# A row-wise NaN maximum: the second tile's load in four strided DMAs, one of them ahead of the first tile's

## Chip, cores and metric

The kernel runs on one core of a Trainium2 chip. The metric is the device time of one execution in microseconds; the runs give the median of several.

## What is computed

The input is 32 x 2048 x 2048 float32 numbers (512 MiB), of which about a tenth are NaN. The output is the maximum of each row of 2048 numbers with NaNs left out, 65536 numbers in all.

```python
batch, seq, dim = 32, 2048, 2048
x = np.random.randn(batch, seq, dim).astype(np.float32)
mask = np.random.rand(batch, seq, dim) < 0.1
x[mask] = np.nan

def reference(x, axis):          # axis = -1
    return np.nanmax(x, axis=axis).astype(np.float32)
```

## The kernel before

The 65536 rows are cut into six groups of tiles (`GROUPS`, from the list `TILES`). In a group each of the 128 partitions holds consecutive rows of the input. A tile is given in quarters of a row (`Q` = 512 numbers, 2 KB): the first tile of the kernel has 4 quarters in each partition (one row, 8 KB, 1 MB in all), the second and nearly all others have 28 (seven rows, 56 KB in each partition, 7 MB in all); the last tiles are cut finer. Three buffers `xt0` to `xt2` take turns.

Each tile goes through four steps. SyncE loads it by one or more DMAs (`load`, line 246). ScalarE reads the upper halfwords of the numbers and writes 16-bit keys to a buffer `kt` (line 270). GpSimd, or now and then ScalarE, turns the keys back into halfwords in which a NaN has become a very low number, and writes them over the old ones in `xt` (lines 280 and 270). VectorE takes the maximum of each row (`tensor_reduce`, line 287). A tile is cut into two or three pieces for this, so that the steps of one tile overlap.

The order on each engine is written out by the program, and the class `Order` places the semaphores: `add` gives an instruction the waits that it needs and an event (a semaphore's name and its count) that others can wait for. A DMA adds 16 to its semaphore. `load` takes one of 14 semaphores (`LANES`) in turn, and a load into a buffer waits until VectorE has read the tile that was in it.

The first three loads, one for each buffer, wait for nothing. They are issued in a block of their own (lines 255 to 264) ahead of the main part, one DMA over all 128 partitions each, and their events stand in the list `ahead`. The main loop takes an event out of `ahead` for each of the first three tiles and issues loads of its own from the fourth on. ScalarE's first piece of a tile waits for the event of its load.

At the end the maxima are stored by six DMAs (line 503).

Of the kernel before, what the change touches and what calls it, by code (L numbers as in the profile page):

```python
# [184 lines left out]
def kernel(  # L185
# [15 lines left out]
    nc = tc.nc  # L201
# [28 lines left out]
    def maxima(lo, hi):  # L230

        if hi <= early:
            return acc0[:, lo:hi]
        assert lo >= early
        return acc1[:, lo - early : hi - early]

    order = Order(nc)
    lanes = [[] for _ in range(LANES)]
    turn = 0

    def load(out, source, deps):
        nonlocal turn
        e = order.add(
            "sp",
            nc.sync,
            lambda: nc.sync.dma_start(out=out, in_=source),  # L246
            deps + lanes[turn],
            lane=f"load{turn}",
            step=16,
        )  # L250
        lanes[turn] = [e]
        turn = (turn + 1) % LANES
        return e

    with tc.tile_critical():  # L255
        xg = xr[P * rows[-1] : P * (rows[-1] + rows[0])].rearrange("(p s) d -> p (s d)", p=P)
        ahead = []
        base = 0
        for xt, ((c,), _, _) in zip(xts, GROUPS[0]):
            c *= Q  # L260
            ahead.append(load(xt[:, :c], xg[:, base : base + c], []))
            base += c
    tc.close()
    tc.compile()  # L264

# [10 lines left out]
    def pool(deps, pair=None, **kw):  # L276
        return order.add(
            "pool",
            nc.gpsimd,
            lambda: nc.gpsimd.tensor_scalar(**kw),  # L280
            deps,
            lane=pair,
            joint=pair is not None,
        )

    def dve(deps, do, **kw):
        return order.add("dve", nc.vector, lambda: do(**kw), deps)  # L287

    def find(deps, acc):
        return dve(  # L290
            deps,
            nc.vector.scalar_tensor_tensor,
            out=acc,
            in0=acc,
            scalar=LEAST,
            in1=acc,
            op0=ALU.is_ge,
            op1=ALU.mult,
        )

    def find_late(deps, acc, none):
        e = pool(
            deps,
            out=none,
            in0=acc,
            scalar1=LEAST,
            scalar2=float(0x00400000),
            op0=ALU.is_lt,
            op1=ALU.mult,
        )  # L310
        bits = acc.bitcast(i32)
        return order.add(
            "pool",
            nc.gpsimd,
            lambda: nc.gpsimd.tensor_tensor(out=bits, in0=bits, in1=none, op=ALU.add),  # L315
            [e],
        )
# [19 lines left out]
    for gi, (s, g) in enumerate(zip(rows, GROUPS)):  # L337
        if gi == len(GROUPS) - 1:
            r0 = 0
        xg = xr[r0 : r0 + P * s].rearrange("(p s) d -> p (s d)", p=P)  # L340
        og = of[r0 : r0 + P * s].rearrange("(p s) -> p s", p=P)
        r0 += P * s
        first = sum(rows[:gi])
        acc = maxima(first, first + s)
        base = 0
        for loads, pieces, reds in g:
            assert sum(loads) == total(pieces) == sum(reds)
            xt, before = xts[number % BUFS], free[number % BUFS]
            number += 1
            landed = []  # L350
            at = 0
            for c in loads:
                c *= Q
                if ahead:
                    e = ahead.pop(0)
                else:
                    e = load(xt[:, at : at + c], xg[:, base + at : base + at + c], before)
                landed.append((at, at + c, e))
                at += c
            clean = []  # L360
            after = []
            at = done = 0
# [27 lines left out]
            def name(i):  # L390
                return f"pair{number}_{pairs[i][0]}" if i in pairs else None
# [15 lines left out]
            for parts in pieces:  # L407
                parts = parts if isinstance(parts, tuple) else (parts,)
                c = int(sum(map(abs, parts))) * Q
                here = [l for a, b, l in landed if a < at + c and b > at]  # L410
                kold = []
                if used + c > KEYS:
# [9 lines left out]
                    out=kts[key][:, used : used + c],  # L422
                    in_=xt[:, at : at + c].bitcast(i16)[:, 1::2],
# [6 lines left out]
                for c in parts:  # L430
                    on = more.pop(0)
                    back, wait, c = c < 0, isinstance(c, float), int(abs(c)) * Q
# [7 lines left out]
                    else:  # L440
                        group.append((at - c, used - c, key))
                        if not on:
                            assert all(k == key for _, _, k in group)
                            lo, klo, _ = group[0]
                            e = pool(
                                [e_key],
                                name(piece),
                                out=xt[:, lo:at].bitcast(i16)[:, 1::2],
                                in0=kts[key][:, klo:used],
                                scalar1=-1.0,  # L450
                                scalar2=float(TOP),
                                op0=ALU.mult,
                                op1=ALU.add,
# [5 lines left out]
                    while reds and done + reds[0] <= min([at] + open_):  # L459
# [8 lines left out]
                        else:  # L468
                            m = max(n // D, 1)
                            to = acc[:, row : row + m]  # L470
                        e = dve(
                            [e for a, b, e in clean if b > lo and a < done] + part,
                            nc.vector.tensor_reduce,
                            out=to,
                            in_=xt[:, lo:done]
                            .bitcast(f32)
                            .rearrange("p (c d) -> p c d", c=m),
                            axis=mybir.AxisListType.X,
                            op=ALU.max,
# [13 lines left out]
        else:  # L493
            e = find(after, maxima(lo, flagged))
            ready += [e] * (gi + 1 - len(ready))
        if gi == len(GROUPS) - 1:
            e = find_late(late_after, late_acc, late)
            ready[LATE] = e
    for (og, bits), e in zip(stores, ready):
# [5 lines left out]
            lane="store",  # L505
            step=16,
# [38 lines left out]
```

## Time and profile before

| what | value |
|---|---|
| time, median of 3 runs | 1250.57 us (1250.36 to 1250.6) |
| span of the profiled execution, first to last instruction | 1248.8 us |
| time of that execution beyond its span | not given by the profile; the median is 1.77 us above the span |
| VectorE (DVE) busy | 1110.5 us, 89% |
| ScalarE (ACT) busy | 968.8 us, 78% |
| GpSimd (POOL) busy | 1164.9 us, 93% |
| DMA queue of the loads, share of 16 engines | 537.14 MB, 99.6% |

The profile is one execution. A row of a timeline has the start, the time taken, the engine, the line, the operation, its output and input, and in brackets the idle time of the engine before it with what ended it. The chain is the work that ended last, followed back from the end; a row of it has the start, the length and what it was. A row of the waits says who waited for whom: total time, number, longest. A row of the windows has the stretch, its length, the busy time of VectorE, ScalarE and GpSimd with instruction counts, the granted clock, the share of time in which the 16 DMA engines were busy, and GB/s. A packet's bytes are counted in the window in which it starts, so very short windows jump. A row of the DMA issues has the count, the KB of one and the time from issue to landing.

### The profile page before, as it was taken

To read this page: it belongs to the slowest core of one execution; us is meant where nothing else is said; L and a number is where in the kernel's file an instruction comes from. 1 tells how busy PE (TensorE), PEld (TensorE's weight loads), DVE (VectorE), ACT (ScalarE), POOL (GpSimd) and SP (SyncE) were. 2 spreads that over 40 slices of the span, in tenths; PEclk is the share of its full clock that TensorE was granted. 3 is DMA by queue.
4 is the path that set the end of the run, shared out by engine and by line. 5 is a ranking of instruction groups with operands and counts; after the bars stand their busy time and mean duration, and the time that the engine had idled before them with its cause. 6 is when DMAs were issued, how large, how long until landed. Compare 5 with 4: busy or idle time off the path is not lost.

```text
span 1248.8 us, 884 instructions
## 1 busy us (share of the span) xinstructions
DVE 1110.5 (89%) x181; ACT 968.8 (78%) x280; POOL 1164.9 (93%) x238
## 2 busy tenths in 40 slices
DVE  0888989888889888898988888988888989999999
ACT  3777887778777877788777877777777779989998
POOL 2999989998999899998999899999999999999998
DMA  9999999999999999999999999999999999999998
GB/s 416 441 413 439 441 441 425 428 441 441 428 425 441 441 435 417 441 441 439 426 428 441 439 432 422 441 441 435 419 439 441 435 430 432 429 432 427 431 428 326
DMA packets 16855, 537.20 MB, mean 430 GB/s; under 512 B 2640, under 2 KB 2640, under 8 KB 4944
## 3 DMA queue, kind: packets, MB, share of 16 engines
q1 hardware_dynamic: 16848, 537.14, 99.6%
q14 instruction: 7, 0.06, 0.0%
HBM read 536.87 MB, written 0.26 MB: 430 GB/s over the span
## 4 chain that ended last, share of the span: by engine, by line
DVE 38%; DMA 36%; POOL 17%; ACT 9%; issue 1%; SPq 0%
DMA xt<-in_x_dram 36%; DVE acc L287 22%; POOL xt L280 17%; DVE lead L287 16%; ACT kt L270 8%; ACT xt L270 1%; SPq L246 0%; SPq L264 0%; SPq L255 0%
## 5 line engine op out<-in xcount | busy, mean ns | idle before, releaser
L280 POOL TENSOR_SCALAR xt<-kt 128x6144 int16<-128x6144 uint16 (+9 forms) x232 | 1163.8, 5016 | 80.5 <-ACT kt L270 67.1
L270 ACT ACTIVATE kt<-xt 128x3584 uint16<-128x3584 int16 (+10 forms) x248 | 913.0, 3720 | 271.8 <-DMA xt<-in_x_dram 250.3
L287 DVE TENSOR_REDUCE acc<-xt 128x3 f32<-128x6144 f32 (+3 forms) x119 | 896.2, 7571 | 132.9 <-POOL xt L280 125.6
L287 DVE TENSOR_REDUCE lead<-xt 128x1 f32<-128x2048 f32 (+3 forms) x59 | 212.9, 3690 | 0.5 <-POOL xt L280 0.5
L270 ACT ACTIVATE xt<-kt 128x512 int16<-128x512 uint16 (+4 forms) x30 | 57.1, 1913 | 0.6
L270 ACT ACT_TABLE_LOAD x1 | 1.3, 1283 | 3.3 <-PEq L264 3.3
L319 DVE MEMSET lead<- 128x1 f32 x1 | 0.1, 59 | 3.4 <-PEq L264 3.4
L287 DVE SCALAR_TENSOR_TENSOR acc<-acc 128x414 f32<-128x414 f32 x1 | 1.2, 1178 | 0.0
L280 POOL TENSOR_SCALAR lead<-lead 128x91 int32<-128x91 f32 x1 | 0.6, 551 | 0.1
L315 POOL TENSOR_TENSOR lead<-lead 128x91 int32<-128x91 int32 x1 | 0.4, 376 | 0.1
L526 POOL MEMSET const-float32-0.0<- 128x1 f32 x1 | 0.1, 99 | 0.2 <-issue 0.2
L270 ACT ACTIVATE lead<-lead 128x1 f32<-128x1 f32 x1 | 0.2, 203 | 0.0
L287 DVE SCALAR_TENSOR_TENSOR lead<-lead 128x7 f32<-128x7 f32 x1 | 0.2, 168 | 0.0
L526 POOL MEMSET const-bfloat16-1.0<- 128x1 bf16 x1 | 0.1, 102 | 0.0
L526 POOL MEMSET const-uint8-127<- 128x1 uint8 x1 | 0.1, 102 | 0.0
L526 POOL MEMSET const-float32-1.0<- 128x1 f32 x1 | 0.1, 99 | 0.0
## 6 DMA issues: line engine op xcount, KB each, us to landing
xt<-in_x_dram SPq DMA_DIRECT2D x61, 7168.0 KB, 22.6
xt<-in_x_dram SPq DMA_DIRECT2D x3, 4096.0 KB, 18.6
xt<-in_x_dram SPq DMA_DIRECT2D x5, 2048.0 KB, 27.5
xt<-in_x_dram SPq DMA_DIRECT2D x3, 3072.0 KB, 25.5
xt<-in_x_dram SPq DMA_DIRECT2D x2, 4352.0 KB, 16.5
xt<-in_x_dram SPq DMA_DIRECT2D x3, 2816.0 KB, 23.3
xt<-in_x_dram SPq DMA_DIRECT2D x2, 3584.0 KB, 25.2
xt<-in_x_dram SPq DMA_DIRECT2D x5, 1024.0 KB, 27.6
```

The source lines that it names most:

```text
L270: lambda: nc.scalar.activation(**kw),
L280: lambda: nc.gpsimd.tensor_scalar(**kw),
L287: return order.add("dve", nc.vector, lambda: do(**kw), deps)
L315: lambda: nc.gpsimd.tensor_tensor(out=bits, in0=bits, in1=none, op=ALU.add),
L319: e_warm = order.add("dve", nc.vector, lambda: nc.vector.memset(warm, 1.0), [])
L526: nc = _bacc.Bacc("TRN2", target_bir_lowering=False, num_devices=1)
```

## The change

The second tile's load becomes four DMAs over strided partitions: partitions 0, 8, 16, ... (16 rows of 56 KB), 4, 12, 20, ... (16 rows), 2, 6, 10, ... (32 rows) and 1, 3, 5, ... (64 rows). The first of them is issued in front of the first tile's load, the other three behind it, and then the third tile's load as before. A helper `first` issues the four; they share one semaphore, and the event that stands in `ahead` for the second tile is the last one's (count 64), so that whoever waits for it waits for all four. Bytes, buffers and everything after these loads stay as they were.

```diff
+    def first(out, source):
+        return order.add(
+            "sp",
+            nc.sync,
+            lambda: nc.sync.dma_start(out=out, in_=source),
+            [],
+            lane="first",
+            step=16,
+        )
...
         ahead = []
         base = 0
+        heads = []
         for xt, ((c,), _, _) in zip(xts, GROUPS[0]):
             c *= Q
-            ahead.append(load(xt[:, :c], xg[:, base : base + c], []))
+            heads.append((xt[:, :c], xg[:, base : base + c]))
             base += c
+        first(*[a[0::8] for a in heads[1]])
+        ahead.append(load(*heads[0], []))
+        for at, step in ((4, 8), (2, 4), (1, 2)):
+            e = first(*[a[at::step] for a in heads[1]])
+        ahead.append(e)
+        ahead.append(load(*heads[2], []))
```

## The prediction

> **What bounds the kernel now.** I read the page from the top: span, engines, the slices, the DMA queues.
>
> ```profile
> span 1248.8 us, 884 instructions
> DVE 1110.5 (89%) x181; ACT 968.8 (78%) x280; POOL 1164.9 (93%) x238
> DMA  9999999999999999999999999999999999999998
> q1 hardware_dynamic: 16848, 537.14, 99.6%
> ```
>
> The 16 DMA engines are busy for 99.6% of the span. No compute engine is, though POOL's 93% is near. Busy shares are averages, so the stretches come next, with the DMA share and GB/s last in each row.
>
> ```profile
> 100.00:400.00 300.00, 267.63 (x37) 227.69 (x56) 284.97 (x52) 1.00 1.00 434
> 400.00:800.00 400.00, 357.79 (x48) 306.51 (x74) 379.68 (x69) 1.00 1.00 435
> 1100.00:1200.00 100.00, 100.00 (x26) 91.78 (x37) 89.97 (x25) 1.00 1.00 430
> 1200.00:1240.00 40.00, 40.00 (x19) 39.63 (x35) 38.31 (x20) 1.00 1.01 422
> ```
>
> The stream runs at 434 GB/s from end to end: its rate is the kernel's rate. VectorE is full as well from 1100 us. What started that run is in the chain of waits that ended last; behind it stands the row of the waits that says how tiles begin.
>
> ```profile
> 999.14 21.81 DMA xt<-in_x_dram
> 1020.95 0.02 issue
> 1020.97 5.33 ACT kt L270
> ...
> 1040.75 33.88 DVE lead L287 x8
> ...
> 1079.63 163.72 DVE lead L287 x49
> ```
> ```profile
> ACT kt L270 <- DMA xt<-in_x_dram: 250.3, 62, 15.0
> ```
>
> VectorE's closing run hangs on a landing at 1020.95 us, and ScalarE waited 62 times for a landing, so tiles start when their data come. Every landing from the second tile on stands behind the second tile's bytes in one full stream. If those bytes take X longer, all later landings, and the end, move by X. The same holds for a gain. The question is what the altered front of the stream costs or saves.
>
> **The front as it is.** The chain in the first 60 us gives SyncE's three issues; the DMA issues of the first 50 us give time to landing; ScalarE's timeline gives its first pieces.
>
> ```profile
> 0.95 0.37 SPq L246
> ...
> 1.38 0.42 SPq L246
> ...
> 1.85 37.53 DMA xt<-in_x_dram
> 39.39 0.02 issue
> 39.41 3.20 ACT kt L270
> ```
> ```profile
> xt<-in_x_dram SPq DMA_DIRECT2D x1, 1024.0 KB, 4.6
> ```
> ```profile
> 5.55 1.91 ACT L270 ACTIVATE kt<-xt 128x2048 uint16<-128x2048 int16 x1 [0.76 <-DMA xt<-in_x_dram]
> 22.47 3.19 ACT L270 ACTIVATE kt<-xt 128x3584 uint16<-128x3584 int16 x1 [15.01 <-DMA xt<-in_x_dram]
> ```
>
> Issues go out at 0.95, 1.38 and 1.85 us. The first tile lands at 0.95 + 4.6 = 5.55, the second at about 22.45, the third at 39.39 us. The last two are 7168 KB apart: 39.39 - 22.45 = 16.94 us, or 433 GB/s. Shared by 16 engines, each moves its 8 of the 128 partition rows (56 KB each) in 16.94 us, **2.12 us a row**. The first tile's 1024 KB would take 2.42 us at that rate.
>
> Short windows show the slow start.
>
> ```profile
> 0.00:1.90 1.90, 0.00 (x0) 0.00 (x0) 0.20 (x4) 1.00 0.00 0
> 1.90:2.50 0.60, 0.00 (x0) 0.00 (x0) 0.00 (x0) 1.00 1.19 232
> 2.50:3.00 0.50, 0.00 (x0) 0.00 (x0) 0.00 (x0) 1.00 0.80 295
> 5.00:22.00 17.00, 2.29 (x1) 1.91 (x1) 2.46 (x1) 1.00 1.00 435
> ```
>
> No byte moves before 1.90 us. Then 0.60 us at 232 instead of 435 GB/s loses 0.60 x (1 - 232/435) = 0.28 us, and 0.50 us at 295 loses 0.16 us: **0.44 us** in all.
>
> **The change part by part.**
>
> *The first issue.* It still goes out at about 0.95 us, but asks for 16 rows of 56 KB in place of 128 rows of 8 KB: one long row for each engine, if all 16 take part. Long rows may cover the slow first reads; at best all 0.44 us come back, at worst none, and the stagger could grow by as much. I take a gain of 0.2 us, half of what is lost. The issue itself took 1.0 us to first byte (0.95 to about 1.95) for 128 rows; nothing in the trace shows that fewer rows shorten this, and more than the 1.0 us cannot be saved.
>
> *Three more issues.* By the two rows above one takes 0.37 to 0.42 us plus some 0.05 us between them. Six instead of three end at about 0.95 + 6 x 0.47 = 3.8 us. The queue then holds at least 0.9 MB of the first strided DMA and 1 MB of the first tile, over 4 us of work from 1.95 us, so the DMA engines don't run dry. If the cover were gone, the price would be three issues, 1.4 us. Completion counts of three more DMAs are a few tiny writes; I cost them at nothing.
>
> *The first tile moves back* by 0.43 us of issue, and its bytes stand behind 16 rows: its landing goes from 5.55 to some 7.5 to 10 us. Behind it are ScalarE's first piece (idle 15.01 us after it), POOL's and VectorE's, and SyncE's next issue, the fourth tile's, which waits for VectorE to release the buffer:
>
> ```profile
> 10.04 2.29 DVE L287 TENSOR_REDUCE acc<-xt 128x1 f32<-128x2048 f32 x1 [6.62 <-POOL xt L280]
> 12.36 0.33 SPq L246 DMA_DIRECT2D xt<-in_x_dram  x1
> ```
>
> Issued at 12.36 us, it isn't served before the third tile is in, at 39.39 us. Moved to some 17 us it keeps over 20 us of cover; nothing is lost. The second tile's pieces now wait for all four DMAs; before, they waited for all of one. No other queue is passed: POOL and ScalarE issue no DMA.
>
> *The same 7168 KB in 16, 16, 32 and 64 rows.* This is the disputed term. Every load in the trace goes over 128 partitions. That each of 16 engines runs 27 GB/s beside the 15 others may be the engine's limit or that of the place in the on-chip memory that it writes to; with 128 rows the two can't be told apart, as each engine may have a place to itself. With every 8th partition, 16 engines write 16 rows in an order that no row of the trace covers. Lower bound: the limit is the engine's, 2.12 us a row, cost 0. Upper bound: throughout the 128 rows two engines share the room of one, 4.24 us a row; each engine has 1 + 1 + 2 + 4 = 8 rows, cost 8 x 2.12 = 16.94 us. I take sharing for the two 16-row DMAs and none for the other two: one row per engine, 8 partitions apart, is furthest from the 128-row loads, while 32 and 64 rows still step finely over the whole width and are nearest to them. Cost: 2 x 2.12 = **4.2 us**.
>
> [...]
>
> Sum: -0.2 + 4.2 = +4.0 us. The profiled span of 1248.8 us becomes 1252.8. The median of the runs, 1250.57, lies 1.77 us above that span; the page has no other time for that execution, and I keep these 1.77 us. **Forecast: 1254.6 us.**
>
> **The rivals.** 0.2% is 2.5 us, about what a measurement of this kernel can tell from no change; slower then means above 1253.1, faster below 1248.1 us.
>
> *A, nothing is shared.* The limit is the engine's and 16 engines take part in each DMA. Only the start changes: -0.2 us, 1250.4 us (1250.1 to 1251.0). For it: the steady 434 GB/s over every stretch, which looks like a fixed engine rate. Against it: each of those rows has the same 128-partition shape. It decides from the point where two 16-row DMAs together cost under 2.7 us instead of 4.2 us: then the kernel is not slower by my bound.
>
> *B, all four are shared.* If the rows of the 32- and 64-row DMAs are dealt out in consecutive runs, two per engine and four per engine, then neighbouring engines start 8 partitions apart there too, as in the 16-row DMAs, and walk in step. Cost 16.94 - 0.2: 1267.3 us. If only the 32-row DMA joins, it is two more rows, 4.2 us: 1258.8; if only the 64-row one joins, 8.5 us: 1263.1. For it: the engines start their rows together, and two that share are slowed alike and stay in step. Against it: nothing shows how rows are dealt out, and the 64-row DMA steps only two partitions.
>
> *C, fewer engines.* The DMAs over 16 rows don't use all engines. If eight carry two rows each in both, they fall 2 x 2.12 = 4.2 us behind the others, and a load counts as landed only with its last row. That is the forecast's time by another way. If the first DMA loads one half and the third issue the other, all engines stay level: that is A. [...]
>
> *D, faster.* This needs 2.5 us, but the start has 0.44 us lost rate and 1.0 us of issue latency, and the stream is otherwise full. Only a rate above 434 GB/s for strided rows would do it, and nothing in the trace goes there.
>
> **How the numbers follow.** Forecast, C included: 0.38, its own range 1253.5 to 1256.0 (no startup gain and a stagger as large on top, or a part of the second shared DMA overlapped by rows of its neighbours). A: 0.21. B: 0.38, about two thirds of it with all four shared. D: 0.03. No case but D may be left out if 8 in 10 are to be held, so the range runs from A's lower end to B's upper end: 1250.0 to 1267.6 us. Slower by over 0.2%: forecast and B, 0.76. Within: A, 0.21. Faster: D, 0.03.
>
> **What would show it.** In the timeline after, ScalarE's piece on the second tile should start at about 26.5 us instead of 22.47, and the third tile's about 16.94 us behind it, at 43.4. The first tile's piece should start near 9.8 us; at 7.5 us it says that 16 rows took the plain 2.12 us, which is A. Short windows of the DMA should show about half of 435 GB/s where the 16-row DMAs run and 435 elsewhere; half of it for over 30 us is B. SyncE's six issues should end before 4 us, with no gap in the stream. From 100 us on, all rows should be as before, moved by the same amount. A second tile that lands late without the end moving by as much would break the step that carries the delay 1:1; a changed rate in the middle of the kernel would break the whole account.

## The result and the profile after

The changed kernel takes **1255.45 us** (median, 1255.42 to 1255.71); the kernel before, run beside it, takes 1250.43 us. The ratio is 1.0041, 95% interval [1.003, 1.0052]: slower by 5.0 us, where 4.0 us was forecast (1254.6 us).

The page of the changed kernel:

```profile
span 1254.4 us, 887 instructions
DVE 1110.5 (89%) x181; ACT 968.8 (77%) x280; POOL 1164.7 (93%) x238
q1 hardware_dynamic: 16896, 537.14, 99.5%
```

Busy times and bytes are those of before; the span is 5.6 us longer, the median 5.0 us. These differ because each profile is one execution: in every run that lists both, the time lies 1.26 to 1.36 us above the span, so the profiled execution of the kernel before took about 1250.1 us (an estimate), 0.3 us less than the median of its runs, and that of the changed kernel 1255.71 us, 0.3 us more than its median. What is read from two traces is therefore some 0.6 us larger than what the medians say. The DMA engines count as busy all the time, so what was lost shows as rate. The windows of the changed kernel (DMA share and GB/s last):

```profile
2.00:6.00 4.00, 0.00 (x0) 0.03 (x1) 0.00 (x0) 1.00 1.07 229
6.00:10.00 4.00, 0.06 (x1) 1.46 (x2) 0.00 (x0) 1.00 1.37 383
10.00:16.00 6.00, 0.00 (x0) 1.91 (x1) 1.20 (x1) 1.00 0.81 225
16.00:26.00 10.00, 2.29 (x1) 0.00 (x0) 1.26 (x1) 1.00 1.03 447
100.00:400.00 300.00, 268.11 (x37) 228.97 (x55) 285.62 (x52) 1.00 1.00 434
```

Two stretches run at about half of 434 GB/s: the first, when only the 16-row DMA from partition 0 is in, and the one from 10 us, behind the first tile's load, when the 16-row DMA from partition 4 is. Between and after them the rate is nearly or fully there; from 16 us on the 32 and 64 rows come at 447 GB/s. A packet counts in the window in which it starts, so windows this short are rough: in the kernel before, 10 to 15 us gives 367 and 15 to 22 us 483 GB/s. The time that the rows take is the better measure. From 1.9 to 4 us the changed kernel's trace has 16 packets (packets, MB, share of 16 engines):

```profile
q1 hardware_dynamic: 16, 0.92, 203.2%
```

These are the 16 rows of the first DMA. All of them start in these 2.1 us, side by side, and their times add up to 203.2% of 16 x 2.1 us: 4.27 us a row, where a row of the steady stream takes 2.12 us. From 100 us on nothing has changed.

ScalarE's timeline shows when tiles one, two and three began; the chain gives SyncE's issues, the third tile's landing, and the landing and last VectorE instruction at the end. The last row is the end of the chain of the kernel before.

```profile
12.80 1.91 ACT L287 ACTIVATE kt<-xt 128x2048 uint16<-128x2048 int16 x1 [5.33 <-DMA xt<-in_x_dram]
...
28.97 7.12 ACT L287 ACTIVATE kt<-xt 128x3584 uint16<-128x3584 int16 x2 [14.26 <-DMA xt<-in_x_dram]
...
45.85 7.12 ACT L287 ACTIVATE kt<-xt 128x3584 uint16<-128x3584 int16 x2 [4.08 <-DMA xt<-in_x_dram]
```
```profile
0.95 0.63 SPq L245
...
1.64 0.56 SPq L256
...
2.25 0.52 SPq L245
...
2.81 0.88 SPq L245
...
3.73 0.59 SPq L245
...
4.37 41.47 DMA xt<-in_x_dram
```
```profile
1004.70 21.89 DMA xt<-in_x_dram
1026.59 0.02 issue
...
1252.77 0.17 DVE lead L304
```
```profile
1247.16 0.17 DVE lead L287
```

The third tile's landing moved from 39.39 to 4.37 + 41.47 = 45.84 us, by 6.4 us; the landing that starts VectorE's closing run from 1020.95 to 1026.59, by 5.6 us; the last VectorE instruction by 5.6 us, too.

### The profile page after: what moved, and what is told of

It is laid out like the page before. It is cut to its first block, busy times and chain, and to the rows that moved or that the text cites. A ratio compares the mean times of both kernels' runs of the same rounds, so it can differ in the third digit from the quotient of the medians.

```text
span 1254.4 us, 887 instructions
## 1 busy us (share of the span) xinstructions
DVE 1110.5 (89%) x181; ACT 968.8 (77%) x280; POOL 1164.7 (93%) x238
## 3 DMA queue, kind: packets, MB, share of 16 engines
q1 hardware_dynamic: 16896, 537.14, 99.5%
## 4 chain that ended last, share of the span: by engine, by line
DVE 38%; DMA 36%; POOL 17%; ACT 9%; issue 1%; SPq 0%
DMA xt<-in_x_dram 36%; DVE acc L304 22%; POOL xt L297 17%; DVE lead L304 16%; ACT kt L287 8%; ACT xt L287 1%; SPq L245 0%; SPq L256 0%; SPq L281 0%; SPq L265 0%
## 6 DMA issues: line engine op xcount, KB each, us to landing
xt<-in_x_dram SPq DMA_DIRECT2D x3, 4096.0 KB, 18.6
```

## The experiments

All times are medians, beside 1250.44 us for the kernel before on the same chip (1250.59 us for the last one). Edits are to the changed kernel's front; `heads` holds the three tiles' buffers and sources. Theory P is the forecast's: what limits is the place in the on-chip memory that is written to.

**The split without the move.**

```diff
-        first(*[a[0::8] for a in heads[1]])
         ahead.append(load(*heads[0], []))
-        for at, step in ((4, 8), (2, 4), (1, 2)):
+        for at, step in ((0, 8), (4, 8), (2, 4), (1, 2)):
```

> The first tile's load goes out first again, then the second tile in the same four strided DMAs (every 8th, 4th, 8, then 4 and 2). Theory P (rows 8 partitions apart make two engines share one way into the on-chip memory, each 16-row DMA costs 2.12 us more, and rows of neighbouring DMAs that overlap with them are slowed a little): the two 16-row DMAs remain, 4.2 to 5.2 us, 1254.6 to 1255.6 us. Rival M (part of the loss is the place in front: the late start of single engines, the slow first rows): about 1 us less than the changed kernel, 1254.4 us or below; and if all of it is the place, 1250.4 us.

Measured: 1254.85 us, ratio 1.0037 [1.0023, 1.005], 4.4 us over before. The split alone brings most of the loss; P's range held. The remaining 0.6 us to the changed kernel would be the place in front, but the intervals overlap, so the two times alone don't show it.

**The move without 16-row DMAs.**

```diff
-        first(*[a[0::8] for a in heads[1]])
+        first(*[a[0::4] for a in heads[1]])
         ahead.append(load(*heads[0], []))
-        for at, step in ((4, 8), (2, 4), (1, 2)):
+        for at, step in ((2, 4), (1, 2)):
```

> No 16-row DMA: every 4th partition (32 rows) in front, then the first tile, then the other 32-row DMA and the 64 rows of every 2nd. P: 32 rows 4 apart and 64 rows 2 apart reach every place, nothing is shared: 1250.0 to 1250.9 us, the second tile lands at 22.0 to 22.8 us. Rival N (a DMA over fewer than 128 partitions costs time in itself, or splitting does): two 32-row DMAs cost about as much as two 16-row ones, 1254 us or above.

Measured: 1251.02 us, ratio 1.0005 [0.9996, 1.0013]. The loss is gone but for 0.6 us, which the interval does not tell from nothing, so neither cutting a load up nor fewer than 128 rows costs it. The time is just above P's range, the second tile's piece began at 23.22 us instead of by 22.8, and the third tile's start in this kernel's ScalarE timeline is 0.71 us later than the 39.41 us of before:

```profile
40.12 7.12 ACT L287 ACTIVATE kt<-xt 128x3584 uint16<-128x3584 int16 x2 [4.10 <-DMA xt<-in_x_dram]
```

**The order alone.** The whole second tile as one DMA in front of the first tile's load.

```diff
-        first(*[a[0::8] for a in heads[1]])
+        e = first(*heads[1])
         ahead.append(load(*heads[0], []))
-        for at, step in ((4, 8), (2, 4), (1, 2)):
-            e = first(*[a[at::step] for a in heads[1]])
```

> The order alone: the whole second tile (one DMA, 128 partitions) is issued in front of the first tile's load, nothing is split. P: no cost in the stream; the second tile lands at 20 to 20.5 us, the first tile right behind it; long rows in front save 0 to 0.4 us of the slow start: 1250.0 to 1250.6 us. Rival Q (the first tile's compute, moved back behind the second tile's data, delays GpSimd, which is nearly full in every tile): up to 2 us more, 1252 us.

Measured: 1250.71 us, ratio 1.0002 [0.9993, 1.0011]: no difference that the times show, and none of the gain that I had for long rows in front. Rival Q, with up to 2 us more, falls. In ScalarE's timeline of this kernel:

```profile
39.99 7.12 ACT L285 ACTIVATE kt<-xt 128x3584 uint16<-128x3584 int16 x2 [2.31 <-DMA xt<-in_x_dram]
```

The third tile starts 0.58 us later than before. In both kernels with long rows in front it is later, by 0.6 to 0.7 us, where 0 to 0.4 us earlier was expected. These are single executions, though, set against a quick one of the kernel before; the medians are later by 0.3 us (whole tile) and 0.6 us (32 rows). From 1.9 to 4 us the traces have the first 16 rows. The first line is that of the kernel with 32 rows in front, the second that of this one.

```profile
q1 hardware_dynamic: 16, 0.92, 136.5%
```
```profile
q1 hardware_dynamic: 16, 0.92, 142.8%
```

That is 2.87 and 3.00 us a row: more than the steady 2.12 us, and far from the 4.27 us of every 8th partition.

**The same row counts in blocks of partitions.**

```diff
-        first(*[a[0::8] for a in heads[1]])
+        first(*[a[0:32] for a in heads[1]])
         ahead.append(load(*heads[0], []))
-        for at, step in ((4, 8), (2, 4), (1, 2)):
-            e = first(*[a[at::step] for a in heads[1]])
+        for lo, hi in ((32, 64), (64, 128)):
+            e = first(*[a[lo:hi] for a in heads[1]])
```

> Same count of rows as 32, 32 and 64, but in blocks of consecutive partitions (0 to 31 in front, the first tile, 32 to 63, 64 to 127). P: a block reaches only half of the places or fewer, so two or more engines share each all through the tile: at least 16.9 us more, 1267 us, and up to some 50 us more if the rows are dealt to the engines in turn, so that four engines meet. Rival N16 (only DMAs of 16 rows are slow, where the rows lie doesn't matter): 1250 to 1251 us. Rival H (the step between the rows in the input is what is slow, 8 partitions being far apart there): consecutive rows are nearest, 1250 to 1251 us.

Measured: 1269.05 us, ratio 1.0149 [1.013, 1.0167], 18.6 us over before. Its windows:

```profile
2.00:10.00 8.00, 0.06 (x1) 1.49 (x2) 0.00 (x0) 1.00 1.03 215
22.00:40.00 18.00, 0.21 (x1) 0.00 (x0) 0.00 (x0) 1.00 1.01 213
42.00:56.00 14.00, 1.52 (x1) 12.02 (x3) 11.00 (x3) 1.00 1.06 459
```

Partitions 0 to 31, and the 64 from 64 to 127, come at half the rate to the end; the next whole tile is at full rate again. The row counts are those of the kernel with every 4th partition in front, which lost 0.6 us at most: where the rows lie decides, not how many there are. The two-engines bound of 16.94 us was met and passed by 1.7 us; the 50 us case was not. Rival N16 falls, and so does H, as consecutive partitions read consecutive rows.

**Four 16-row DMAs instead of two.**

```diff
-        for at, step in ((4, 8), (2, 4), (1, 2)):
+        for at, step in ((4, 8), (2, 8), (6, 8), (1, 2)):
```

> The 32-row DMA of every 4th partition is cut into two 16-row DMAs of every 8th (2, 10, ... and 6, 14, ...), so four 16-row DMAs instead of two; the rest as in the changed kernel (1255.45 us). Theory P: each 16-row DMA of this step costs 2.1 us more than its rows at the full rate, so 4.2 us on top: 1259.2 to 1260.2 us. Rival E (the loss lies at the two seams, with the first tile's load and with the 32-row DMA, or in issuing): one more issue and no new kind of seam, under 1 us more, 1255.5 to 1256.5 us.

Measured: 1260.36 us, ratio 1.008 [1.0064, 1.0095]: 4.9 us above the changed kernel, 0.2 us over the top of P's range and far from E's. The cost goes with the number of 16-row DMAs, some 2.5 us each.

**The same partitions, consecutive input rows.** The second tile's rows then stand in other partitions, and their maxima in other places of the output.

```diff
-        first(*[a[0::8] for a in heads[1]])
+        xt1, xg1 = heads[1]
+        first(xt1[0::8], xg1[0:16])
         ahead.append(load(*heads[0], []))
-        for at, step in ((4, 8), (2, 4), (1, 2)):
-            e = first(*[a[at::step] for a in heads[1]])
+        for at, step, lo, hi in ((4, 8, 16, 32), (2, 4, 32, 64), (1, 2, 64, 128)):
+            e = first(xt1[at::step], xg1[lo:hi])
```

> The four DMAs write the same partitions as in the changed kernel, but read consecutive rows of the input (0 to 15, 16 to 31, 32 to 63, 64 to 127), so that only the step on the input's side is gone; the second tile's rows stand in other partitions, and their maxima in other places of the output. P: the way into the on-chip memory is what is shared, 1254.9 to 1255.9 us as in the changed kernel. Rival H (16 streams at a step of 8 partitions' rows, some 6.5 MB, disturb each other in the input's memory): the loss goes, 1250.4 to 1251.2 us.

Measured: 1255.28 us, ratio 1.0038 [1.0023, 1.0053], as the changed kernel. Taking away the step on the input's side changes nothing, so the loss is on the side that is written; rival H falls here, too.

**896 KB by themselves.** The front of the kernel before, with one DMA more: 896 KB of the third tile behind the first tile's load. The third tile's own load waits for it and writes the same bytes again.

```diff
-        first(*[a[0::8] for a in heads[1]])
         ahead.append(load(*heads[0], []))
-        for at, step in ((4, 8), (2, 4), (1, 2)):
-            e = first(*[a[at::step] for a in heads[1]])
-        ahead.append(e)
-        ahead.append(load(*heads[2], []))
+        xt2, xg2 = heads[2]
+        e = first(xt2[:, : 7 * D // 8], xg2[:, : 7 * D // 8])
+        ahead.append(load(*heads[1], []))
+        ahead.append(load(*heads[2], [e]))
```

This is the DMA over all partitions; the two others have `xt2[0::8], xg2[0::8]` and `xt2[0:16], xg2[0:16]` in the line of `e`.

> The loads as in the kernel before, and one more DMA behind the first tile's load: 896 KB of the third tile over all 128 partitions (7 KB of each), which the third tile's own load, made to wait for it, writes again. It prices an added 896 KB by itself. All theories: 2.1 us of the stream, up to 2.6 with a seam: 1252.5 to 1253.1 us.

> The same frame and the same 896 KB, but as 16 rows of every 8th partition. P: 4.2 us, up to 5 with the seams: 1254.7 to 1255.5 us, 2.1 us or more above the one over all partitions. Rival E (loss from the cutting up of the second tile, not from the 16 rows themselves): as over all partitions, 1252.5 to 1253.1 us.

> The same frame with the added 896 KB as 16 rows of consecutive partitions, 0 to 15. P, with ways that four neighbouring partitions have in common: 16 rows fall on four ways, four engines on each, 4 x 2.12 = 8.5 us: 1258.9 to 1259.6 us. Rival N16 (16 rows cost double wherever they lie): 4.2 us, 1254.7 to 1255.5 us.

| added 896 KB | time | over before | ratio, 95% interval |
|---|---|---|---|
| 128 partitions, 7 KB each | 1252.62 us | 2.2 us | 1.0017 [1.0008, 1.0027] |
| 16 rows, every 8th partition | 1254.97 us | 4.5 us | 1.0037 [1.0024, 1.005] |
| 16 rows, partitions 0 to 15 | 1258.92 us | 8.3 us | 1.0066 [1.0047, 1.0086] |

The same bytes cost about one, two and four times 2.1 us. The windows of the second and the third kernel give the rates behind the first tile's load:

```profile
5.00:9.00 4.00, 0.00 (x0) 0.00 (x0) 0.00 (x0) 1.00 1.09 254
```
```profile
5.00:13.00 8.00, 0.00 (x0) 0.00 (x0) 0.00 (x0) 1.00 1.23 211
```

The first is a little over half rate, its edges in full-rate neighbours. The second counts packets of the next load that start at its end, so its rate says little; the time does: 0.92 MB in 8.3 us is 110 GB/s, a quarter. In the packet records of the two traces the 16 rows start within 0.6 us and last 3.9 to 4.4 us each in the second kernel, 6.6 to 7.8 us in the third.

## Why the prediction came out

**What bounds it: right.** Busy times stayed, and the end moved by what the landings moved. The carry of 1:1 holds from 1020.95 us on (5.6 and 5.6 us). Up to there it seems not exact: 6.4 us at the third tile had become 5.6. The packet records settle this. A load ends with 16 packets of 4 bytes, which start when its last rows end. The third tile's start from 38.62 to 39.03 us before and from 44.14 to 45.43 us after; on average they moved by 5.73 us. Those of the landing at 1020.95 us start from 1019.50 to 1020.59 us before and from 1024.88 to 1026.24 us after; on average they moved by 5.66 us. So the stream kept its delay within 0.1 us. The last of the 16 started at 39.03 us before and at 45.43 us after, and the landings stand at 39.39 and 45.84 us: a landing waits for the last. The distance from the first to the last grew from 0.4 to 1.1 us in the kernel before, while it was 1.3 to 1.4 us all along in the changed one; that is where the 0.8 us went.

**The disputed term: right in place and nearly in size.** Two 16-row DMAs at half rate were forecast, 2 x 2.12 = 4.2 us, the other two DMAs at full rate. In the trace the first 16 rows took 4.27 us each and the second 16 took 4.25 us, 2.15 and 2.13 us too long, and the windows give 229 and 225 GB/s. Four such DMAs instead of two double the loss, 32 rows in place of 16 remove it, and the added 896 KB price it at 4.53 - 2.18 = 2.35 us each. The blocks of partitions ran at 213 to 215 GB/s for 32 and 64 rows and at 110 GB/s for 16. The forecast's factor of two was an estimate of its author: no row of the kernel before shows it. What the runs show in its place are these times of a row, 4.27 and 4.25 us beside 2.12.

**The start, and what the sum left out.** The step "I take a gain of 0.2 us" for long rows in front has failed, and the forecast was 1.0 us short. The packet records of the two traces show where the rest lies. A packet of the steady stream takes 0.31 us for 8 KB and 2.12 us for 56 KB. What each engine lost against this up to the third tile, on average over the 16, is in the table.

| | before | changed | difference |
|---|---|---|---|
| first packets start at | 2.08 us | 2.57 us | 0.48 us |
| first tile's 8 KB packets, beyond 0.31 us each | 0.46 us | 0.81 us | 0.35 us |
| first 16 rows, beyond 2.12 us | | 2.15 us | 2.15 us |
| second 16 rows, beyond 2.12 us | | 2.13 us | 2.13 us |
| first 16 rows of the 32-row DMA, beyond 2.12 us | | 0.63 us | 0.63 us |

The sum is 5.7 us, the 5.73 us by which the third tile moved. The slow start was sized well: 0.46 us where the short windows gave 0.44. The 16 long rows in front, at half rate anyway, lost no more by it, but they started 0.48 us later, and that ate the gain. The larger term left out is the seams: packets that run beside the half-rate rows are slow as well. From 6.2 to 8.1 us the first tile's packets took 0.58 us each, and the first rows of the 32-row DMA 2.75 us, which is some 0.7 and 0.6 us per engine. The forecast had only named this as a way to the top of its range. Without the place in front a part of it remains: with the split alone the loss was 4.4 us, 0.2 us over the two terms, and the third tile moved by more:

```profile
44.16 7.12 ACT L286 ACTIVATE kt<-xt 128x3584 uint16<-128x3584 int16 x2 [4.08 <-DMA xt<-in_x_dram]
```

That is ScalarE's row of the split-only kernel: 44.16 - 39.41 = 4.75 us, half a microsecond beyond 4.24 us. The table is one execution of each kernel, and their times differ by 0.6 us more than the medians.

The whole range, 1250.0 to 1267.6 us, holds every rival but D, so it proves little that the time lies in it. What speaks for the account is that the narrow range of 1253.5 to 1256.0 us held and that the experiments found the loss where the forecast had put it, in the 16-row DMAs over every 8th partition.

**The times of single steps.** ScalarE's piece on the second tile began at 28.97 us instead of the forecast 26.5, the first tile's at 12.80 instead of 9.8: a load lands with its last packet. Of the first 16 rows, 15 started from 2.37 to 2.75 us and one only at 3.92, and of the 16 packets that end the first tile's load, 15 started from 9.65 to 10.64 us and the last at 11.89. The first tile's delay cost nothing, as said. SyncE's issues took 0.52 to 0.88 us, not 0.37 to 0.42, and the sixth began at 4.37 us instead of ending before 4; but for the one late row the stream had work all the while. The 1.77 us between span and median were not the time of an execution beyond its span, which is about 1.3 us: the median and the span came from different executions. The forecast adds 4.0 us to the median by this, so the sum does not suffer.

**The rivals.** A (nothing shared) fell with the half-rate windows. B (all four shared) fell with the full rate from 16 us on, 447 GB/s. In consecutive runs a 32-row DMA of every 4th partition would begin with the rows of partitions 0, 8, 16, ..., the set that took 4.27 us a row; in the kernel that has this DMA in front the first 16 rows took 2.87 us each, no more than the 3.00 us with the whole tile in front, so the rows are not dealt out that way. For blocks of partitions the half rate did go on to the last row, 213 GB/s from 22 to 40 us. How the rows are dealt to the engines was not determined. C (fewer engines, with two rows each) would give the same time as the forecast, but eight engines with two rows in turn would start eight rows, 2.12 us each, and then eight more; the trace has all 16 under way at once, at 4.27 us each. So C falls as it was put. That rows to some sets of partitions go at half or a quarter of their speed, side by side, is shown: 225 and 229 GB/s for every 8th partition, 213 and 215 for blocks of 32 and 64, 110 for one of 16, where the steady stream has 434. That two or four engines share one way into the memory, and that four neighbouring partitions have a way in common, are the author's inference from these rates; no view here shows the ways themselves.

## What to carry to other kernels

In these runs a DMA's rate goes by which partitions it writes, so the price of a piece is its bytes over the rate that its partitions reach: all 128, every 4th or every 2nd ran at the full 434 GB/s or so, every 8th at 225 to 229 and a block of 32 or 64 at 213 to 215, about half of it, a block of 16 at 110, a quarter. The stream of loads was full (99.5% of the span), and what was lost early was lost at the end: 5.73 us at the third tile, 5.66 us at the landing that starts VectorE's closing run. A small transfer put early into such a stream is better cut along the free dimension, where 896 KB cost 2.2 us, or over every 4th partition, where the split and the move together cost 0.6 us, which is not told from nothing, than over every 8th (4.5 us for 896 KB) or over 16 neighbouring partitions (8.3 us). What ran beside the slow rows was slowed as well, for as long as they lasted: the first tile's packets took 0.58 us each instead of 0.31, the first rows of the 32-row DMA 2.75 us instead of 2.12.

## What the hardware showed unexpectedly

Long rows first in the stream did not hide its slow start: with the whole second tile in front the first 16 rows took 3.00 us each, 0.88 us over the steady 2.12, where the kernel before lost 0.46 us on its 8 KB packets. In one execution of each, this difference of 0.4 us is most of the 0.58 us by which the third tile began later; the medians differ by 0.3 us, less than the interval.

SyncE's issue of a load with strided partitions took longer, 0.52 to 0.88 us in the changed kernel, than the 0.37 to 0.42 us of whole tiles before; the first tile's unstrided load issued behind a strided one took 0.56 us as well. It is the step between the partitions and not the number of rows: in the kernel with blocks of partitions the chain gives these issues, of partitions 0 to 31, of the first tile (line 256) and of partitions 32 to 63.

```profile
0.95 0.40 SPq L245
...
1.41 0.41 SPq L256
...
1.86 0.43 SPq L245
```

With the same strided partitions and consecutive input rows it stayed at 0.52 to 0.62 us, so the step on the input's side isn't the cause. The three kernels that open with every 8th partition have their first packet at 2.35 to 2.37 us, the one that opens with every 4th at 2.29, and all others at 1.95 to 1.99 us. Why the issue takes longer was not tried.
